# An encoder layer on one core: the second chunk's projection takes its weight quarters two at a time

## Chip, cores, metric

One core of a Trainium2 chip. The metric is the device time of one execution of the whole kernel in microseconds, the median over runs. The engines are named as the profile names them: PE (TensorE; PEld its weight loads), ACT (ScalarE), DVE (VectorE), POOL (GpSimd), SP (SyncE, whose queue issues the DMAs).

## What is computed

One encoder layer on two groups of tokens (1024 prompt and 256 sample tokens, each group with 16 meta tokens ahead), model width 2048, all in float32:

```python
def encoder_layer(h, norm_w, w_in, q_norm_a, k_norm_a, q_norm_b, k_norm_b, rpb, w_out, rope_tabs):
    u = rms_norm(h, norm_w) @ w_in                       # 2048 -> 52 strips of 128 columns
    qa, ka, va, za, qb, kb, vb, zb = jnp.split(u, split_points(), axis=-1)
    qa = apply_axial_rope(rms_norm(qa, q_norm_a), rope_tabs)      # 8 heads
    ka = apply_axial_rope(rms_norm(ka, k_norm_a), rope_tabs)      # 2 key/value heads
    ya = global_gqa(qa, ka, va) * jax.nn.silu(za)
    qb, kb = rms_norm(qb, q_norm_b), rms_norm(kb, k_norm_b)       # 8 heads
    yb = neighbourhood_attention(qb, kb, vb, rpb) * jax.nn.silu(zb)
    return h + jnp.concatenate([ya, yb], axis=-1) @ w_out
```

## The kernel before

**Arithmetic.** A float32 product is made of three matmuls on operands that are split into a high and a low part: high by high, high by low, low by high. `split` does it for a weight tile: ACT casts `wr` to the high part `wh` (line 66), DVE subtracts it for the low part `wl` (line 67). Activations `x` are kept split in SBUF.

**Chunks.** The tokens go in two chunks. Chunk one (sample tokens and the first part of the prompt) is projected up to about 600 us, chunk two (the other 784 prompt tokens) from there to 1758 us, and the output projection with its own sums (`products`, lines 1070 to 1072, PSUM tile `pq`) follows to the end. Chunk two's tokens are two blocks: 512 tokens (tile `x`) and 272 (tile `xb`). Its projection shares PE with the attention: first the eight global heads (about 640 to 1310 us), then, from 1310 us on, the eight local (neighbourhood) heads, whose scores and values are hung in between the strips by `run_due`.

**Strips.** `project` makes one strip of 128 output columns of `w_in` (a key, query, value or gate strip of a head) by `strips(jobs, getx)`. The first strip of chunk two is a joint one, with two jobs (`KA`, `VA`); the others have one. The contraction over 2048 rows is 16 k-tiles, in four quarters `c` of `WCH` = 4 k-tiles. Per quarter SP loads 256 KB of weights into a `wr` buffer (pool `raw`), ACT makes `wh` (a cast or copy) and DVE makes `wl`; for strips whose low part was kept from chunk one, SP loads `wl` from DRAM (`wld`, line 210) instead. The pool `w` has four buffers of `wh` and four of `wl`, so four quarters fit. Then for each token block `b` twelve matmuls (4 k-tiles by 3) go into that block's PSUM tile `pp`: 12 with 512 columns and 12 with 272 in each quarter, four times per strip. In the last strip (`turn`) the 272 block goes first.

**Behind a strip.** Keys and queries are squared (`ms`, ACT, line 260), summed over partitions on POOL, scaled by a root (`rs_l`, `rs_r`) and stored to DRAM, from where `qfull` and `kfull` are read back. Values are scaled (`vt`, DVE, line 289) and transposed on PE (`tp`, line 540); these transposes are ordered behind a certain place of the next strip, told by `tie` = (quarter, block). `z` is the gate strip.

**What sets the order.** Tile's scheduler sets the order of each engine's instructions from its own model of time; each engine runs its list in that order. Buffers of a pool come free when their last reader is through. At the end of chunk two the first `ww` tiles (weights of the output projection, line 1037) and the first `yf` (attention outputs, line 987, in the `raw` pool) are loaded, cast and split into `wm` and `yh`/`yl`, on the same ACT, DVE and SP lists; `behind_v` orders the splits of the fifth to sixteenth `wm` behind the last `vt`.

Of the kernel before, what the change touches and what calls it, by code (L numbers as in the profile page):

```python
# [48 lines left out]
WCH = 4  # L49
# [10 lines left out]
class Kern:  # L60
# [131 lines left out]
    def strips(self, jobs, getx):  # L192


        nc, tc = self.nc, self.tc
        out = [[pool.tile([P, 512], F32, tag=tag, name="pp") for pool, tag in pools] for _, _, pools in jobs]
        for c in range(KT // WCH):
            ws = []
            behind = self.behind.pop(0) if self.behind else None
            for j, (s, _, _) in enumerate(jobs):  # L200
                wp = self.w if j < 2 else self.w1
                with tc.high_priority(offset=self.woff), tc.issue_after(behind) if behind else nullcontext():
                    w = self.raw.tile([P, WCH, P], F32, tag="raw", name="wr")
                    cuts = ((0, 1), (1, WCH)) if self.projected == 3 and c == 0 and not self.second else ((0, WCH),)
                    for i, e in cuts:
                        self.lastw = nc.sync.dma_start(w[:, i:e], self.io["w_in"][s][:, c * WCH + i:c * WCH + e, :]).ins
                    wh = wp.tile([P, WCH, P], F32R, tag="wh", name="wh")
                    wl = wp.tile([P, WCH, P], F32R, tag="wl", name="wl")
                    if self.second and s not in AGAIN:
                        nc.sync.dma_start(wl[:].bitcast(F32), self.wld[s][:, c * WCH:(c + 1) * WCH, :])  # L210
                        nc.scalar.copy(wh[:], w[:])
                    else:
                        for i, e in cuts:
                            self.lastsplit = self.split(wh[:, i:e], wl[:, i:e], w[:, i:e])
                            self.lasthi = self.hi
                ws.append((wh, wl))
                if not self.second and s not in AGAIN:
                    nc.sync.dma_start(self.wld[s][:, c * WCH:(c + 1) * WCH, :], wl[:].bitcast(F32))
            nb = len(jobs[0][1])
            for b in range(nb)[::-1] if self.turn else range(nb):  # L220
                for k in range(WCH):
                    kt = c * WCH + k
                    xh, xl = getx(kt)[b]
                    first, last = kt == 0, kt == KT - 1
                    for (wh, wl), ps, (_, blocks, _) in zip(ws, out, jobs):
                        p, n = ps[b], blocks[b][1]
                        nc.tensor.matmul(p[:, :n], wh[:, k, :], xh[:, :n], start=first, stop=False)  # L227
                        nc.tensor.matmul(p[:, :n], wh[:, k, :], xl[:, :n], start=False, stop=False)  # L228
                        self.lastmm = nc.tensor.matmul(p[:, :n], wl[:, k, :], xh[:, :n], start=False, stop=last).ins  # L229
                if self.turned and (c, b) == self.tie:  # L230
                    for i in self.turned:
                        tc.add_manual_dep(i, self.lastmm.name, mybir.DependencyInfo(
                            mybir.DependencyClass.NoSync, mybir.DependencyReason.DATA), reason="turned")
                    self.turned = []
            if c % 2:
                self.run_due()
        return out
# [527 lines left out]
    def chunk2(self):  # L765
# [20 lines left out]
        def k_strip(s, g, wc, rope):  # L786
            k, km = k_first(g)

            def evac(ps):
                for p, (o, n) in zip(ps, BL):  # L790
                    rp = (ct[:, o:o + n], st[:, o:o + n]) if rope else None
                    self.qk_evac(p, o, n, wc, rp, [(0, n, k[:, 0, C1P + o:C1P + o + n], k[:, 1, C1P + o:C1P + o + n])])
                return k, km
            return s, BL, evac

        def v_rows_of(s, g):

            def evac(ps):
                for p, (o, n) in zip(ps, BL):
                    self.rows_out(self.v_rows(p, o, n), n, self.vn[g], C1P + o)  # L800
            return s, BL, evac

        def v_tiles(g):

            h, l = (self.v.tile([P, 8, P], F32R, tag=f"v{i}", name="va", align_bytes=ALIGN) for i in range(2))
            nc.sync.dma_start(l[:].bitcast(F32), self.vn[g][:].rearrange("(t p) d -> p t d", p=P))
            nc.scalar.copy(h[:], l[:].bitcast(F32))
            nc.vector.tensor_tensor(out=l[:], in0=l[:].bitcast(F32), in1=h[:].bitcast(F32), op=ALU.subtract)
            return [(h[:, j, :], l[:, j, :]) for j in range(8)], self.load_vm(g)
# [12 lines left out]
        def q_strip(s, h, wc, rope):  # L822
            q = self.q.tile([P, 2, NP], F32R, tag="q", name="q", align_bytes=ALIGN)
            nc.sync.dma_start(q[:, :, :C1P].bitcast(F32), self.qd[h][:])

            def evac(ps):
                for p, (o, n) in zip(ps, BL):
                    rp = (ct[:, o:o + n], st[:, o:o + n]) if rope else None
                    self.qk_evac(p, o, n, wc, rp, [(0, n, q[:, 0, C1P + o:C1P + o + n], q[:, 1, C1P + o:C1P + o + n])])
                return q  # L830
            return s, BL, evac

        def z_strip(s, h):
            z = self.z.tile([P, NP], F32, tag="z", name="z")
            nc.sync.dma_start(z[:, :C1P], self.zd[h][:, :C1P])

            def evac(ps):
                for p, (o, n) in zip(ps, BL):
                    self.z_evac(p, o, n, [(0, n, z[:, C1P + o:C1P + o + n])])
                return z  # L840
            return s, BL, evac
# [39 lines left out]
        def run(h, q, z, k, v):  # L881
            (k, km), (v, vm) = k, v
            for b in range(4):
                c = slice(QB * b, QB * b + QB)
                keys = [(k[:, 0, o:o + P], k[:, 1, o:o + P]) for o in range(0, NP, P)]
                for _ in self.attend(q[:, :, c], z[:, c], keys, km, v, vm[:], self.yd[0][:, 2 * b:2 * b + 2, h, :]):
                    pass
# [51 lines left out]
        def fill(n):  # L939
            for _ in range(min(n, len(late))):  # L940
                pr(late.pop(0))

        for g in range(2):
            if g == 0:
                k, _ = pr(k_strip(KA, 0, kw, True), v_rows_of(VA, 0))
                self.tie = 0, 1
            else:
                k, = pr(k_strip(KA + g, g, kw, True))
                pr(v_rows_of(VA + g, g))
            v = v_tiles(g)  # L950
            for h in range(4 * g, 4 * g + 4):
                z, = pr(z_strip(ZA + h, h) + (((self.sp, "sp"),) if h == 0 else ()))
                q, = pr(q_strip(QA + h, h, qw, True))
                run(h, q, z, k, v)
                fill(FILL)
# [2 lines left out]
            f(0)  # L958
        self.due = iter(local_heads())
        fill(len(late) - 1)  # L960
        self.turn, self.tie = True, (1, 0)
        fill(1)
        load_z(NH - 1)
        self.due = iter([[(0, f, (NH - 1, b)) for f, b in ((values, n - 2), (scores, n)) if 0 <= b < 4] for n in range(6)])
# [381 lines left out]
```

## Time and profile before

| | |
|---|---|
| runs | 2155.97, 2157.99, 2158.89 us; median 2157.99 |
| the profiled execution | 2156.31 us, of which the span is 2154.5 |
| PE busy | 2147.4 us, 11745 matmuls |
| DVE, ACT, POOL busy | 1666.1, 1190.9, 524.0 us |
| mean clock granted to PE | 1.00 |

Times in the rows are us from the span's start. A row of the timeline gives start, length, engine, line, operation and tiles (out<-in), and in brackets how long the engine sat idle before it and what ended that. Matmuls overlap: one of 512 columns has a length of about 0.39 us, while the next starts 0.23 us later, so what a stretch costs PE is read from starts. A row of the waits gives the sum, the number and the longest. The prediction shows the lines that it uses.

### The profile page before, as it was taken

How to read it: one execution, taken by the hardware profiler on the slowest of the kernel's cores; microseconds unless marked ns; L12 is line 12 of the kernel's file. 1: busy time of each engine (PE TensorE's matmuls, PEld its weight loads, DVE VectorE, ACT ScalarE, POOL GpSimd, SP SyncE). 2: the span in 40 equal slices, each digit the busy share in tenths (PEclk: the TensorE clock that was granted, in tenths of full speed). 3: DMA queues.
4: the chain of work that ended last, by engine and by line, in shares of the span. 5: the costliest groups of instructions: out<-in, count | busy, mean ns of one | idle time of the engine just before them, and what ended most of it. 6: DMA issues, size and time to landing. Idle time of an engine off the chain costs nothing.

```text
span 2154.5 us, 34001 instructions
## 1 busy us (share of the span) xinstructions
PE 2147.4 (100%) x11745; PEld 1878.4 (87%) x11745; DVE 1666.1 (77%) x3013; ACT 1190.9 (55%) x2419; POOL 524.0 (24%) x250
## 2 busy tenths in 40 slices
PE   9999999999999999999999999999999999999999
PEld 7888888888888999998999999989999888888887
DVE  7698977788874899996799988777787786545763
ACT  7677644454665777776677775444444454232230
POOL 1142422222221223231133224333333311000000
PEclk9999999999999999999999999999999999999999
DMA  8666789988654333334233244554433364762663
GB/s 294 215 193 220 238 291 320 341 280 281 212 191 133 97 102 106 110 97 142 91 110 100 95 129 150 184 161 135 138 124 123 114 215 140 242 234 91 234 225 107
DMA packets 257420, 377.24 MB, mean 175 GB/s; under 512 B 43072, under 2 KB 108768, under 8 KB 257248
## 3 DMA queue, kind: packets, MB, share of 16 engines
q1 hardware_dynamic: 257248, 375.07, 53.7%
q8 instruction: 92, 1.51, 0.3%
q14 instruction: 80, 0.66, 0.1%
HBM read 281.01 MB, written 100.38 MB: 177 GB/s over the span
## 4 chain that ended last, share of the span: by engine, by line
PE 98%; DVE 1%; DMA 1%; SPq 0%; issue 0%; ACT 0%; DVEq 0%
PE pp L229 22%; PE pp L227 22%; PE pp L228 22%; PE pq L1072 6%; PE pq L1070 6%; PE pq L1071 6%; PE po L519 2%; PE sp L485 2%; PE sp L378 1%; PE sp L379 1%; PE po L420 1%; PE sp L377 1%; PE po L419 1%; PE po L418 1%; PE tp L540 0%; PE sm_ps L316 0%
## 5 line engine op out<-in xcount | busy, mean ns | idle before, releaser
L227 PE MATMUL pp<-x,wh 128*128 128x512 f32 (+1 forms) x1664 | 654.0, 394 | 0.6 <-ACT wh L66 0.3
L229 PE MATMUL pp<-x,wl 128*128 128x512 f32 (+1 forms) x1664 | 647.8, 390 | 0.2 <-DVE wl L67 0.2
L228 PE MATMUL pp<-x,wh 128*128 128x512 f32 (+1 forms) x1664 | 647.9, 390 | 0.0
L229 PEld LDWEIGHTS pp<-x,wl 128*128 128x128 f32 x1664 | 312.5, 188 | 61.4 <-DVE wl L67 0.8
L227 PEld LDWEIGHTS pp<-x,wh 128*128 128x128 f32 x1664 | 312.4, 188 | 55.6 <-ACT wh L66 2.0
L228 PEld LDWEIGHTS pp<-x,wh 128*128 128x128 f32 x1664 | 312.9, 188 | 51.9
L262 POOL PARTITION_ALL_REDUCE m<-ms x78 | 223.1, 2860 | 352.5 <-ACT ms L260 300.3
L67 DVE TENSOR_TENSOR wl<-wr,wh 128x512 fp32r<-128x512 f32 (+2 forms) x287 | 209.6, 732 | 107.2 <-ACT wh L66 80.4
L346 POOL PARTITION_ALL_REDUCE tot<-a x80 | 181.0, 2262 | 433.5 <-DVE a L343 419.8
L66 ACT CAST wh<-wr 128x512 fp32r<-128x512 f32 (+2 forms) x287 | 173.5, 611 | 162.5 <-PE pp L228 147.8
L228 PE MATMUL pp<-xb,wh 128*128 128x272 f32 x832 | 240.8, 289 | 0.0
L227 PE MATMUL pp<-xb,wh 128*128 128x272 f32 x832 | 239.6, 288 | 0.0
L229 PE MATMUL pp<-xb,wl 128*128 128x272 f32 x832 | 239.0, 287 | 0.0
L328 POOL PARTITION_ALL_REDUCE ma<-m x80 | 113.3, 1417 | 447.8 <-DVE m L326 436.3
L1072 PE MATMUL pq<-wm,yl 128*128 128x512 f32 x560 | 218.3, 390 | 0.6 <-DVE yl L67 0.6
L1070 PE MATMUL pq<-wm,yh 128*128 128x512 f32 x560 | 218.3, 390 | 0.0
L1071 PE MATMUL pq<-wm,yh 128*128 128x512 f32 x560 | 218.0, 389 | 0.0
L227 PEld LDWEIGHTS pp<-xb,wh 128*128 128x128 f32 x832 | 156.5, 188 | 7.5
L228 PEld LDWEIGHTS pp<-xb,wh 128*128 128x128 f32 x832 | 156.5, 188 | 7.4
L229 PEld LDWEIGHTS pp<-xb,wl 128*128 128x128 f32 x832 | 157.4, 189 | 0.1
L1072 PEld LDWEIGHTS pq<-wm,yl 128*128 128x128 f32 x560 | 105.1, 188 | 22.9 <-DVE yl L67 1.0
L1071 PEld LDWEIGHTS pq<-wm,yh 128*128 128x128 f32 x560 | 105.1, 188 | 21.6
(218 smaller groups left out, 3951.9 us busy)
## 6 DMA issues: line engine op xcount, KB each, us to landing
wr<-in_w_in SPq DMA_DIRECT2D x413, 256.0 KB, 3.5
wld<-wl SPq DMA_DIRECT2D x132, 256.0 KB, 4.3
wl<-wld SPq DMA_DIRECT2D x132, 256.0 KB, 3.1
yr<-yd SPq DMA_DIRECT2D x35, 512.0 KB, 5.2
wq<-in_w_out SPq DMA_DIRECT2D x64, 256.0 KB, 5.1
td<-wq SPq DMA_DIRECT2D x64, 256.0 KB, 4.4
ww<-td SPq DMA_DIRECT2D x64, 256.0 KB, 5.2
ww<-in_w_out SPq DMA_DIRECT2D x48, 256.0 KB, 5.1
```

What stands on the lines that cost most here:

```text
L66: self.hi = nc.scalar.copy(hi, full).ins
L67: return nc.vector.tensor_tensor(out=lo, in0=full, in1=hi.bitcast(F32), op=ALU.subtract).ins
L227: nc.tensor.matmul(p[:, :n], wh[:, k, :], xh[:, :n], start=first, stop=False)
L228: nc.tensor.matmul(p[:, :n], wh[:, k, :], xl[:, :n], start=False, stop=False)
L229: self.lastmm = nc.tensor.matmul(p[:, :n], wl[:, k, :], xh[:, :n], start=False, stop=last).ins
L262: nc.gpsimd.partition_all_reduce(m2[:], ms[:], P, RED.add)
L328: nc.gpsimd.partition_all_reduce(ma[:], m1[:], P, RED.max)
L346: nc.gpsimd.partition_all_reduce(tot[:], a1[:], P, RED.add)
L485: nc.tensor.matmul(dst, k[:, o:o + P], qfv[:, a:e, :], start=True, stop=True)
L1070: nc.tensor.matmul(ps, yh, wh, start=k == 0, stop=False)
L1071: nc.tensor.matmul(ps, yh, wl, start=False, stop=False)
L1072: self.lastmm = nc.tensor.matmul(ps, yl, wh, start=False, stop=k == 7).ins
```

## The change

With one job and more than one token block, an even quarter of a strip only loads its weights and is held; the odd quarter that follows runs both: 24 matmuls for the first block with the two quarters' weights one after the other, then 24 for the second. `tie` is renamed to the pair in which the transposes are to come, since a pair counts by its first quarter.

```diff
         out = [[pool.tile([P, 512], F32, tag=tag, name="pp") for pool, tag in pools] for _, _, pools in jobs]
+        held = []
         for c in range(KT // WCH):
...
+            held.append((c, ws))
             nb = len(jobs[0][1])
+            if nb > 1 and len(jobs) == 1 and c % 2 == 0:
+                continue
             for b in range(nb)[::-1] if self.turn else range(nb):
-                for k in range(WCH):
-                    kt = c * WCH + k
+                for kt, ws in [(d * WCH + k, w) for d, w in held for k in range(WCH)]:
+                    k = kt % WCH
                     xh, xl = getx(kt)[b]
...
-                if self.turned and (c, b) == self.tie:
+                if self.turned and (held[0][0], b) == self.tie:
...
+            held = []
             if c % 2:
                 self.run_due()
         return out
...
-                self.tie = 0, 1
+                self.tie = 0, 0
...
-        self.turn, self.tie = True, (1, 0)
+        self.turn, self.tie = True, (0, 0)
```

Lines of the changed kernel stand five further down behind the edit (line 289 is 294, 540 is 545, 1037 is 1042), and the three matmul lines 227 to 229 are 231 to 233. The order of every engine's instructions is built anew. Each engine has as many of them as before.

The order of PE in one of the first strips (`pp_8007` is its 512 block, `pp_8008` its 272 block; `wh_8011`, `wl_8012` are quarter nought), at the end of that quarter's 512s. Before:

```order
L227 MATMUL pp_8007<-x_6761,wh_8011 128x512
L228 MATMUL pp_8007<-x_6761,wh_8011 128x512
L229 MATMUL pp_8007<-x_6761,wl_8012 128x512
L227 MATMUL pp_8008<-xb_6738,wh_8011 128x272
L228 MATMUL pp_8008<-xb_6738,wh_8011 128x272
L229 MATMUL pp_8008<-xb_6738,wl_8012 128x272
```

And after:

```order
L231 MATMUL pp_8007<-x_6761,wh_8011 128x512
L232 MATMUL pp_8007<-x_6761,wh_8011 128x512
L233 MATMUL pp_8007<-x_6761,wl_8012 128x512
L231 MATMUL pp_8007<-x_6769,wh_8017 128x512
L232 MATMUL pp_8007<-x_6769,wh_8017 128x512
L233 MATMUL pp_8007<-x_6769,wl_8018 128x512
```

The 512s of quarter one (`wh_8017`) follow at once, and the 272s of quarter nought come after them.

The order of DVE in the last strip, between the scaling of the value strip's first block (`vt_20168`) and that of its second (`vt_20178`); `q_20090` is the last query head's split, `wl_20262` is quarter two of the last strip, `wl_20292` (before) and `wl_20268` (after) quarter three, `wm` are output weights. Before:

```order
L67 TENSOR_TENSOR wl_20262<-wr_20259,wh_20261 128x512
L289 TENSOR_TENSOR vt_20168<-pp_20001,rb2_320 128x512
L355 TENSOR_TENSOR tot_19967<-tot_19967,r_20159 128x256
L356 SCALAR_TENSOR_TENSOR r_20159<-tot_19967,r_20159 128x256
L67 TENSOR_TENSOR q_20090<-qfull_20087,q_20090 128x1024
L67 TENSOR_TENSOR wl_20292<-wr_20289,wh_20291 128x512
```

And after:

```order
L294 TENSOR_TENSOR vt_20168<-pp_20001,rb2_320 128x512
L360 TENSOR_TENSOR tot_19967<-tot_19967,r_20159 128x256
L361 SCALAR_TENSOR_TENSOR r_20159<-tot_19967,r_20159 128x256
L67 TENSOR_TENSOR q_20090<-qfull_20087,q_20090 128x1024
L67 TENSOR_TENSOR wl_20262<-wr_20259,wh_20261 128x512
L67 TENSOR_TENSOR wl_20268<-wr_20265,wh_20267 128x512
```

The split of quarter two has moved behind the q split, whose cast ACT likewise does first now. Behind these rows four `wm` splits and then `vt_20178` follow in both.

The order of SP there. Before:

```order
L868 DMA qfull_20087<-q2d15_164 128x784
L987 DMA yf_20352<-yd0_165 128x512
L364 DMA yd1_166<-y_20074 128x4x64
L568 DMA vm3_271<-vmd9_98 48x128
L1037 DMA ww_20355<-in_w_out 128x512
```

And after:

```order
L873 DMA qfull_20087<-q2d15_164 128x784
L369 DMA yd1_166<-y_20074 128x4x64
L573 DMA vm3_271<-vmd9_98 48x128
L992 DMA yf_20352<-yd0_165 128x512
L1042 DMA ww_20355<-in_w_out 128x512
```

`yf_20352` goes into the raw buffer that the split `wl_20262` frees, and the first output weights stand behind it in both.

The order of PE at the transposes of the value strip's second block (`tp_20181`), in the last strip. Before:

```order
L229 MATMUL pp_20190<-x_6825,wl_20262 128x512
L227 MATMUL pp_20191<-xb_6834,wh_20291 128x272
L540 MATMUL tp_20181<-ident_239,vt_20178 128x128 x2
L540 MATMUL tp_20181<-ident_239,vt_20178 16x128
L228 MATMUL pp_20191<-xb_6834,wh_20291 128x272
```

And after:

```order
L233 MATMUL pp_20191<-xb_6858,wl_20268 128x272
L231 MATMUL pp_20190<-x_6801,wh_20261 128x512
L545 MATMUL tp_20181<-ident_239,vt_20178 128x128 x2
L545 MATMUL tp_20181<-ident_239,vt_20178 16x128
L232 MATMUL pp_20190<-x_6801,wh_20261 128x512
```

They stood behind the first 272 of quarter three, and stand now behind the first 512 of the second pair, whose twenty-four 272s come ahead of it.

## The prediction

> **What bounds the kernel now.** I read the page first: busy shares, then the chain that ended last. TensorE (PE) is busy all the time, and 98% of the chain is PE, two thirds of it the projection's three matmul lines. So the time moves only if PE's matmuls come closer together or if PE waits.
>
> ```profile
> PE 2147.4 (100%) x11745; PEld 1878.4 (87%) x11745; DVE 1666.1 (77%) x3013; ACT 1190.9 (55%) x2419; POOL 524.0 (24%) x250
> ...
> PE 98%; DVE 1%; DMA 1%; SPq 0%; issue 0%; ACT 0%; DVEq 0%
> PE pp L229 22%; PE pp L227 22%; PE pp L228 22%; PE pq L1072 6%; PE pq L1070 6%; PE pq L1071 6%; PE po L519 2%; PE sp L485 2%; PE sp L378 1%; PE sp L379 1%; PE po L420 1%; PE sp L377 1%; PE po L419 1%; PE po L418 1%; PE tp L540 0%; PE sm_ps L316 0%
> ```
>
> Then the stretches of PE alone (us, busy with count, clock, DMA share, GB/s). The first two are chunk two: PE busy without a gap at full clock. The third is the output projection, 1325 matmuls of 512 columns in 300.00 us, so 226.4 ns each: the step of an undisturbed run of 512s.
>
> ```profile
> 640.00:1310.00 670.00, 670.00 (x4316) 1.00 0.36 109
> 1310.00:1757.00 447.00, 447.00 (x2688) 1.00 0.46 147
> 1830.00:2130.00 300.00, 300.00 (x1325) 1.00 0.57 198
> ```
>
> Then the waits. From 640 to 1757 us no wait of PE is listed, so inside the strips nothing can be won by bringing data earlier; from 1757 on PE has one. Of the other engines the waits that touch the change are those for a weight slot: SP's and ACT's, which end when PE has used up the quarter that sat there.
>
> ```profile
> PE pq L1072 <- DVE yl L67: 0.6, 1, 0.6
> SPq L210 <- PE pp L229: 341.4, 117, 7.0
> ACT wh L66 <- PE pp L228: 147.8, 96, 4.4
> ```
>
> **The change part by part.** It adds and removes no instruction; 100 pairs of quarters (50 strips of two pairs; the joint strip and chunk one keep their order) run as 24 matmuls of 512 columns and 24 of 272 in place of 12, 12, 12, 12.
>
> *Matmul order.* The place shown in the order lists is 669.53 to 678.02 us in the trace, a pair without attention in it. The joint strip before it already runs 24 and 24, which is a trial of the new order inside this trace (start, modelled length):
>
> ```profile
> 626.36 0.39 PE L227 MATMUL pp<-x,wh 128*128 128x512 f32 x1
> ...
> 631.80 0.29 PE L227 MATMUL pp<-xb,wh 128*128 128x272 f32 x1
> ...
> 634.79 0.40 PE L227 MATMUL pp<-x,wh 128*128 128x512 f32 x1
> ...
> 637.53 0.29 PE L227 MATMUL pp<-xb,wh 128*128 128x272 f32 x1
> ...
> 669.53 0.39 PE L227 MATMUL pp<-x,wh 128*128 128x512 f32 x1
> ...
> 672.28 0.29 PE L227 MATMUL pp<-xb,wh 128*128 128x272 f32 x1
> ...
> 673.78 0.39 PE L227 MATMUL pp<-x,wh 128*128 128x512 f32 x1
> ...
> 678.02 0.39 PE L227 MATMUL pp<-x,wh 128*128 128x512 f32 x1
> ```
>
> Differences of starts: the pair in the present order takes 8.49 us (669.53 to 678.02). Its twelve 512s take 2.75, twelve undisturbed ones 12 x 0.2264 = 2.72: a run of 512s that is entered from 272s loses 0.03 us in its first steps. The twelve 272s take 1.50. In the joint strip 24 and 24 take 8.43 (626.36 to 634.79): 5.44 and 2.99. The run of 512s behind it, entered after twenty-four 272s, takes 2.74, so a longer run of 272s doesn't make the entry dearer. A pair with one entry less should take 2.75 + 2.72 + 2.99 = 8.46, 0.03 less than now; taken whole from the joint strip it is 8.43, 0.06 less.
>
> How many entries go? Counted through the built order of PE, passages from a 272 to a 512 of the projection fall from 156 to 58, since in pairs with attention the attention's matmuls often stand between; passages from attention into a 512 fall from 158 to 126, and into a 272 rise from 129 to 168. The 98 are worth 98 x 0.03 = 2.9 us. For the 32 I have no row that isolates the loss, so I bound it by nothing and by the same 0.03 (1.0 us) and take 0.4. Term: -3.3 us; ends -2.9 and, with the joint strip's 0.06 on all 100 pairs, -6.
>
> The Trainium skill, "TensorE: Matmul & The Clock Gate", section "Back-to-back issue gap", gives an isolated spacing of N/2.4 + 2.5 ns, whatever stands before: 216 ns for 512 columns and 116 for 272. By it a pair would take 24 x (216 + 116) = 7.97 us in either order and this term would be zero; the trace disagrees in the size (8.49) and in that the same twelve 512s take 2.75 or 2.72.
>
> *Weight slots.* Four quarters fit. An even quarter is now held until its 272s are through at 5.45 + 1.50 = 6.95 us of the pair instead of 4.25, so its slot comes free 2.7 us later; an odd one at 8.5 as now, but it is first needed 2.72 us into the pair and not at 4.25, 1.5 us sooner. SP, which waits there 341.4 us with loads of keys, values and later weights queued behind, and ACT, with softmax steps behind a cast, wait up to 2.7 us longer. How early weights stand ready: quarter two of the last strip, whose low half is split by 1741.25 (row below), is first used one pair after the strip's start at 1740.61, near 1749, so 7.7 us early; read by name, the other quarters of chunk two are 6.8 to 20 us early. 2.7 + 1.5 = 4.2 leaves 2.6 at worst. Cost nothing, as long as that margin covers it; if it doesn't, PE waits for `wl`.
>
> *PSUM.* The same two banks per strip are written over the same pair; the 512 bank is finished 3.0 us before the strip's end and not 1.5, so its evacuation can start sooner. Nothing.
>
> *Transposes.* Behind a pair's first 24 matmuls in place of a quarter's 24 they come 5.4 us after a strip's start instead of 4.2. Their readers are copies and a store of value rows, needed a strip later. Nothing, except in the last strip.
>
> *Last strip and handover to the output projection*, the one place where the order of work moves (start, length, engine; waits in brackets). ACT, then SP, DVE and PE:
>
> ```profile
> 1728.27 0.63 ACT L77 ACTIVATE rs_l<-m 128x512 f32<-128x512 f32 x1 [3.22 <-DVE m L263]
> 1729.40 0.24 ACT L561 CAST km<-kfull 128x64 fp32r<-128x64 f32 x1 [0.49 <-DMA kfull<-kfd]
> ...
> 1730.20 0.40 ACT L260 ACTIVATE ms<-pp 128x272 f32<-128x272 f32 x1
> ...
> 1745.62 1.05 ACT L66 CAST q<-qfull 128x1024 fp32r<-128x1024 f32 x1 [1.81 <-DMA yf<-yd]
> ...
> 1748.11 0.62 ACT L66 CAST wm<-ww 128x512 fp32r<-128x512 f32 x1 [0.92 <-PE pp L229]
> 1748.93 1.87 ACT L66 CAST wm<-ww 128x512 fp32r<-128x512 f32 x3 [0.20 <-DMA ww<-in_w_out]
> ```
>
> ```profile
> 1742.74 0.38 SPq L987 DMA_DIRECT2D yf<-yd  x1
> ...
> 1744.20 6.08 SPq L1037 DMA_DIRECT2D ww<-in_w_out  x5
> ```
>
> ```profile
> 1740.58 0.67 DVE L67 TENSOR_TENSOR wl<-wr,wh 128x512 fp32r<-128x512 f32 x1
> ...
> 1746.70 1.23 DVE L67 TENSOR_TENSOR q<-qfull,q 128x1024 fp32r<-128x1024 f32 x1 [1.91 <-ACT q L66]
> 1747.84 0.69 DVE L67 TENSOR_TENSOR wl<-wr,wh 128x512 fp32r<-128x512 f32 x1
> ...
> 1749.24 2.49 DVE L67 TENSOR_TENSOR wm<-ww,wm 128x512 fp32r<-128x512 f32 x4
> 1751.65 0.43 DVE L289 TENSOR_TENSOR vt<-pp,rb 128x272 f32<-128x272 f32 x1
> ...
> 1761.72 0.68 DVE L67 TENSOR_TENSOR yl<-yf,yh 128x512 fp32r<-128x512 f32 x1
> ```
>
> ```profile
> 1740.61 0.42 PE L227 MATMUL pp<-xb,wh 128*128 128x272 f32 x1
> ...
> 1754.11 0.49 PE L540 MATMUL tp<-ident,vt 128*128 128x128 f32 x3
> ...
> 1761.48 0.39 PE L1071 MATMUL pq<-wm,yh 128*128 128x512 f32 x1
> 1762.45 0.50 PE L1072 MATMUL pq<-wm,yl 128*128 128x512 f32 x1 [0.59 <-DVE yl L67]
> 1762.79 0.39 PE L1070 MATMUL pq<-wm,yh 128*128 128x512 f32 x1
> ```
>
> Now: the last strip starts at 1740.61. Quarter two's low weights are split at 1740.58, ahead of the long q split; the raw buffer that this frees lets SP load `yf` at 1742.74 and, behind it in SP's queue, the output weights (`ww`) at 1744.20. Four of them are cast by 1750.80 (6.6 us after the first issue) and split, `vt` ends at 1752.08, and the transposes that read it run at 1754.11, 2 us later: cover that the change uses up.
>
> After: the low split stands behind the q split, `yf` and `ww` behind the low split, `vt` behind four `wm` splits. If q arrives as now, the q split ends at 1747.93, the low one 0.69 later at 1748.6 (PE wants it one pair into the strip, 1740.61 + 8.43 = 1749.0, so it is just in time), `yf` goes then and `ww` 0.45 behind at 1749.05; plus 6.6 to the fourth cast, 0.6 for its split, 0.43 for `vt`: 1756.7. The transposes stand one pair (8.43), 24 matmuls of 272 (2.99), one of 512 (0.23) and four earlier transposes (0.5) behind the strip's start: 1752.8. PE would stand 3.9 us. But ACT's order now puts the square `ms` of the last query strip's second block ahead of the key cast `km`, which waits for a transfer and delays it by 0.6 us (idle 0.49 before 1729.40, and 0.15 to the next start), and DVE's sum `m` of the first block, for which ACT stands 3.22 us until 1728.27, is one place forward. So the chain from that square to q (sum over partitions, root, store, reload, cast) starts earlier: by nothing, or by 0.6 and half of that 3.22, 2.3 together (an estimate). That bounds the stall by 1.6 and 3.9 with `ww` landing as now; with landings as short as the shortest of this kind it shrinks by some 1.2 (2.6 for the 3.8 us of the first one here):
>
> ```profile
> DMA to landing us min/median/max: 2.6/5.1/8.4
> ```
>
> Ends 0.4 and 3.9; I take 1.2, nearer the low one, since the whole chain from that square follows it. Against it stands the one wait of PE: the step from 1761.48 to 1762.45 is 0.97 for 0.227, the next 0.34, together 0.86 lost to a `yl` that DVE split at 1761.72 behind a row of `wm`. The last Z block's 272s now end 2.7 us sooner against the strip's end, so its scaling clears DVE sooner; I take this wait as gone. Handover: 1.2 - 0.9 = +0.3, ends -0.5 and +3.9.
>
> *Sum* against the profiled execution's 2156.31 us (span 2154.5 and 1.8 around it): -3.3 + 0.3 = 2153.3. The median of the runs, 2157.99, is 1.7 above that execution, so 2155.0 for the median.
>
> **The rivals.**
>
> C, larger gain: the whole 0.06 to 0.07 of the joint strip on every pair, and the wait gone: -6 to -7.5, with little of a stall. For it: the joint strip's 24 512s have no entry loss at all. Against: it has two jobs' weights in turn, and attention stands in half the other pairs. 2150.5 to 2152.
>
> A, a new wait in place of the old: q arrives as now and PE stalls 3.9 us at the transposes in the last strip, with the wait at 1762.45 gone or not: -3.3 + 3.9 - 0.4 = +0.2, 2158.2. For it: every link stands in the order. Against: ACT's order starts the chain sooner.
>
> B, no gain: the loss at entry is made up by something else, or the 272s gain what the 512s lose, so a step's mean depends on the columns alone. 0 + 0.3: 2158.3. Against: 2.75 and 2.72 in the trace. The Trainium skill's formula named above would give this result.
>
> D, slower: ACT is held at a weight cast 2.7 us longer, with a softmax step of the global heads behind it, and values come to PE late. It decides as soon as that step has less than 2.7 us of cover. 32 global blocks (8 heads of 4); if one in four loses half of 2.7, 8 x 1.35 = 10.8, less 3.0: 2165.8. For it: ACT waits there 96 times already. Against: no wait of PE in 1117 us, and ACT is busy 55%.
>
> **How the numbers follow.** The three runs spread over 0.14%; 0.2%, 4.3 us, is about what a measurement of this kernel can tell from no change. Forecast 0.48 (2153 to 2157), C 0.20, A 0.14, B 0.10, D 0.08. Faster than 2153.7 are C and a lower edge of the forecast, 0.06: 0.26. Slower is D: 0.08. The rest is same: 0.66. The range takes the forecast, A, B and the near half of C: 2151.5 to 2159.
>
> **What would show it.** The pair at 669.53 takes 8.46 us or a little less; chunk two from 640 to its end is 3 us shorter with PE still 100% busy; no PE wait before 1740; one on `vt` of about 1 us at the last strip's transposes; none on `yl`. I am wrong if entries into 512 still cost what they did per pair, if PE waits for `wl`, softmax or value operands inside strips, or if the `vt` wait is near 4 us.

## The result: slower by 0.16%

The changed kernel takes 2160.32 us (median of 22 runs, 2158.29 to 2163.36) against 2157.02 before (22 runs, 2155.94 to 2160.07): a ratio of 1.0016, 95% interval 1.0011 to 1.0022. The forecast was 2155.0 in a range of 2151.5 to 2159. The profiled executions differ by 4.0 us of span, 2158.5 against 2154.5.

The changed kernel's page, shares and chain. PE's busy time fell by 0.9 us, its share to 99%, and 5% of the chain left PE, for DVE, issue and ACT:

```profile
PE 2146.5 (99%) x11745; PEld 1879.5 (87%) x11745; DVE 1674.9 (78%) x3013; ACT 1188.1 (55%) x2419; POOL 512.6 (24%) x250
...
PE 93%; DVE 3%; issue 1%; ACT 1%; DMA 1%; POOL 0%; SPq 0%; DVEq 0%; POOLq 0%; ACTq 0%
```

Its waits of PE after 600 us, where there had been one of 0.6:

```profile
PE tp L545 <- DVE vt L294: 2.7, 1, 2.7
PE po L521 <- DVE Pm L343: 1.6, 1, 1.6
PE po L425 <- DVE pl L67: 0.8, 2, 0.4
```

PE at the pair whose price the prediction worked out:

```profile
669.40 0.40 PE L231 MATMUL pp<-x,wh 128*128 128x512 f32 x1
...
674.87 0.29 PE L231 MATMUL pp<-xb,wh 128*128 128x272 f32 x1
...
677.86 0.40 PE L231 MATMUL pp<-x,wh 128*128 128x512 f32 x1
```

The pair takes 8.46 us (before 8.49), 5.47 and 2.99, as worked out. PE around the last two strips, starts again, waits in brackets:

```profile
1738.05 0.29 PE L233 MATMUL pp<-xb,wl 128*128 128x272 f32 x1
1739.91 0.36 PE L521 MATMUL po<-Pm,vm 128*128 128x256 f32 x1 [1.57 <-DVE Pm L343]
...
1753.19 0.40 PE L231 MATMUL pp<-x,wh 128*128 128x512 f32 x1
1756.32 0.87 PE L545 MATMUL tp<-ident,vt 128*128 128x128 f32 x3 [2.74 <-DVE vt L294]
1756.85 0.78 PE L232 MATMUL pp<-x,wh 128*128 128x512 f32 x1
1757.42 0.63 PE L233 MATMUL pp<-x,wl 128*128 128x512 f32 x1
1757.85 0.63 PE L231 MATMUL pp<-x,wh 128*128 128x512 f32 x1
```

Two waits, and behind the second the 512s start 0.43 us apart, not 0.227. The stretch of PE from 1756 to 1760 gives the granted clock as 0.57:

```profile
1756.00:1760.00 4.00, 3.68 (x11) 0.57 1.03 368
```

So the slow steps, five of 0.43 behind one of 0.57, go with a lowered clock, and no wait is listed for them. The Trainium skill, "TensorE: Matmul & The Clock Gate", section "Part 1: The HAM clock gate", states that it falls to half after about 3.4 us of idle; the traces disagree: here 2.74 us were enough, and in three of the runs below about 1.9.

Where 4.0 us come from, by starts of matmuls in both traces (chunk two and output projection, 1550.32 us before and 1554.30 after): the strips up to 1721 us are 2.40 shorter in their steps (the 512s 2.98 shorter, the attention's matmuls 0.60 longer); the two waits on `pl`, a low half of the probabilities, cost 1.09; the wait on `Pm` 1.73; that on `vt` 2.91; the slow steps behind it, those of the transposes with them, 1.53; the rest of the handover is 0.88 shorter, 0.75 of it the lost step on `yl`, which is gone. Sum +4.0.

What the wait on `vt` hangs on (DVE, then SP, then ACT):

```profile
1739.35 0.41 DVE L343 TENSOR_TENSOR Pm<-Sm,Pm 16x256 fp32r<-16x256 f32 x1
...
1746.48 1.23 DVE L67 TENSOR_TENSOR q<-qfull,q 128x1024 fp32r<-128x1024 f32 x1 [2.06 <-ACT q L66]
1747.62 1.29 DVE L67 TENSOR_TENSOR wl<-wr,wh 128x512 fp32r<-128x512 f32 x2
...
1752.45 0.69 DVE L67 TENSOR_TENSOR wm<-ww,wm 128x512 fp32r<-128x512 f32 x1 [2.75 <-ACT wm L66]
...
1755.74 0.43 DVE L294 TENSOR_TENSOR vt<-pp,rb 128x272 f32<-128x272 f32 x1
```

```profile
1748.34 0.32 SPq L992 DMA_DIRECT2D yf<-yd  x1
1748.75 4.75 SPq L1042 DMA_DIRECT2D ww<-in_w_out  x9
```

```profile
1751.80 0.62 ACT L66 CAST wm<-ww 128x512 fp32r<-128x512 f32 x1 [4.31 <-DMA ww<-in_w_out]
```

The q split is 0.2 us sooner than before, not 2.3; from there on each link is where the prediction's upper end had it, and `vt` ends at 1756.2 for 1756.7. `Pm` ends at 1739.8 where it ended at 1738.6 before the change, while PE wants it at 1738.2. Before the change PE took it at 1739.5, 0.9 us after it was ready; that was its cover:

```profile
1738.17 0.41 DVE L338 TENSOR_TENSOR Pm<-Sm,Pm 16x256 fp32r<-16x256 f32 x1
```

```profile
1739.53 0.28 PE L516 MATMUL po<-Pm,vm 128*128 128x256 f32 x1
```

### The profile page after: what moved, and what is told of

It is laid out like the page before. It is cut to its first block, busy times and chain, and to the rows that moved or that the text cites. A ratio compares the mean times of both kernels' runs of the same rounds, so it can differ in the third digit from the quotient of the medians.

```text
span 2158.5 us, 34003 instructions
## 1 busy us (share of the span) xinstructions
PE 2146.5 (99%) x11745; PEld 1879.5 (87%) x11745; DVE 1674.9 (78%) x3013; ACT 1188.1 (55%) x2419; POOL 512.6 (24%) x250
## 4 chain that ended last, share of the span: by engine, by line
PE 93%; DVE 3%; issue 1%; ACT 1%; DMA 1%; POOL 0%; SPq 0%; DVEq 0%; POOLq 0%; ACTq 0%
PE pp L232 21%; PE pp L231 21%; PE pp L233 21%; PE pq L1077 6%; PE pq L1076 6%; PE pq L1075 6%; PE po L524 2%; PE sp L490 2%; PE po L425 1%; PE sp L383 1%; PE sp L382 1%; PE sp L384 1%; PE po L424 1%; PE po L423 1%; PE tp L545 0%
## 5 line engine op out<-in xcount | busy, mean ns | idle before, releaser
L351 POOL PARTITION_ALL_REDUCE tot<-a x80 | 169.4, 2118 | 436.6 <-DVE a L348 407.2
L1076 PEld LDWEIGHTS pq<-wm,yh 128*128 128x128 f32 x560 | 105.2, 188 | 21.8
L1075 PEld LDWEIGHTS pq<-wm,yh 128*128 128x128 f32 x560 | 105.1, 188 | 21.7
```

Of the source, the lines that this page charges most:

```text
L351: nc.gpsimd.partition_all_reduce(tot[:], a1[:], P, RED.add)
L1075: nc.tensor.matmul(ps, yh, wh, start=k == 0, stop=False)
L1076: nc.tensor.matmul(ps, yh, wl, start=False, stop=False)
```

## Experiments

Theory 1: the step gain is real, and the new order of the lists of DVE, ACT and SP at the end of chunk two makes the loss. Theory 2: the pairs themselves make it, since PE asks sooner than the others can follow. Beside the timing (ratio to before with its interval), "from 600" is the time from the first matmul on `xb` to the last start on `pq` in the profiled execution, 1550.32 before and 1554.30 after; it leaves out chunk one, whose end lies between 599.7 and 601.4 us in these traces. Strips of chunk two are numbered from 0 (the joint one) to 50 (the last). All kernels that pair only some strips have this edit, with `tie` as before in the others:

```diff
-            if nb > 1 and len(jobs) == 1 and c % 2 == 0:
+            if pair and c % 2 == 0:      # pair: PAIRS(number of the strip)
```

**Which strips.** The last one quarter by quarter (`n < 50`), the last two (`n < 49`), and the last one alone in pairs (`n == 50`):

> All strips of chunk two in pairs except the last one, which goes quarter by quarter as before. In the built order the low split of the last strip's quarter two still stands behind the long q split on DVE, with the attention-output load and the output weights behind it on SP, and the meta probabilities (Pm) still stand behind a weight split of the next strip; only the transposes are back behind the first 272 of quarter three. Theory 1 (the lists of DVE and SP make the loss at the end): the wait on Pm stays at about 1.6 us and the transposes still wait, some 1.2 to 1.8 us, since their place is 1.2 us later and the value scaling as late as in the changed kernel; time about 1 us above before, 2158. Theory 2 (the pair in the last strip makes the loss by asking for the transposes sooner): no wait at the transposes, time about 2156.

> All strips in pairs except the last two. In the built order the low split of the last strip's quarter two stands ahead of the q split again, as before the change. Both theories: no wait at the transposes and no slow clock behind it. Theory 1: the wait on Pm goes too or falls under 0.5 us; what is left is the gain of the matmul order, 2.2 us, less two waits of 0.44 us on a low half of the probabilities (pl) among the global heads: 2155.5 to 2156, 1 to 1.5 us below before. The rival that the entry into a run of 512s costs nothing and the gain in the trace is noise: 2157 or above.

> Only the last strip in pairs, all others quarter by quarter as before. In the built order the low split of its quarter two stands ahead of the q split, the transposes stand where they do in the changed kernel. Theory 1: the value scaling ends near 1752.1 us as before and the transposes, wanted near 1752.8, wait under 0.5 us; the wait of 0.86 us on the low half of y is gone: between 0.9 us below before and no change, 2156 to 2157. Theory 2: the transposes wait 2 to 3 us and the clock falls behind them: 3 us above before, 2160.

| | time, us | ratio | from 600 |
|---|---|---|---|
| last strip apart | 2159.86 | 1.0008 (0.9999 to 1.0017) | 1553.52 |
| last two apart | 2158.30 | 0.9999 (0.9991 to 1.0008) | 1550.55 |
| last alone in pairs | 2155.87 | 0.9992 (0.9983 to 1.0000) | 1549.88 |

Waits of PE after 600 us in the first:

```profile
PE po L524 <- DVE Pm L346: 1.9, 1, 1.9
PE tp L548 <- DVE vt L297: 1.3, 1, 1.3
PE pq L1080 <- DVE yl L68: 1.1, 2, 0.9
PE po L428 <- DVE pl L68: 0.8, 2, 0.4
```

and in the second:

```profile
PE po L524 <- DVE Pm L346: 1.8, 1, 1.8
PE po L428 <- DVE pl L68: 0.8, 2, 0.4
```

In the third none is listed. With the last strip apart the transposes still wait, 1.3 us, inside the bounds of theory 1 (the time is 2.0 us above before for its 1, since `yl` is late again and `Pm` later); with the last strip alone in pairs, and its transposes where the changed kernel has them, they don't wait at all. So the pair in the last strip isn't what makes that wait. Counted from the first matmul on `xb`, `vt` ends at 1156.2 us in the changed kernel and with the last strip apart, at 1152.7 with the last two apart, at 1152.6 with the last alone, and at 1152.1 before the change. What the three have in common with the lists: the low split of quarter two stands behind the q split where strip 49, the one before, is paired, and ahead of it where it is not. A paired strip holds the weight buffer that quarter two needs until near its end; this is the link that the prediction's section on slots had costed at nothing. That the held buffer is why the scheduler moved the row is read from the lists and not shown by a run. The expectation that the wait on `Pm` goes with the second was wrong: it stays, 1.8 us, and the gain in steps (the strips up to the last two are 2.4 us shorter there, waits apart) is spent on it and on `pl`. Seven of the eleven executions of the second have a mean granted clock of 0.999 and take 2157.6 to 2158.6 us; the other four, the profiled one among them, have 1.000 and take 2156.5 to 2157.5. So its median is longer than its trace would have it.

**The opposite dose.** No pairs, and each quarter goes through its blocks in two halves:

```diff
-            for b in range(nb)[::-1] if self.turn else range(nb):
-                for kt, ws in [(d * WCH + k, w) for d, w in held for k in range(WCH)]:
+            parts = ((0, 2), (2, 4)) if self.second and len(jobs) == 1 else ((0, WCH),)
+            for b, (ka, kb) in [(b, p) for p in parts for b in (range(nb)[::-1] if self.turn else range(nb))]:
+                for kt, ws in [(d * WCH + k, w) for d, w in held for k in range(ka, kb)]:
```

> The opposite dose: no pairs, and each quarter of chunk two's single strips goes through its blocks in two halves (6 of 512, 6 of 272, 6, 6), which raises the passages from a 272 into a 512 from 156 to 322. Theory that an entry into a run of 512s costs about 0.03 us, 0.027 of it in the first six steps: 166 x 0.027 = 4.5 us more, 2161.5, with the quarter at 4.28 us for 4.25 where no attention stands between. Rival that a step's mean depends on the columns alone: no change, quarter 4.25 us.

2164.20 us, 1.0028 (1.0017 to 1.0038), from 600 1558.25. A quarter without attention takes 4.27 us:

```profile
669.48 0.40 PE L235 MATMUL pp<-x,wh 128*128 128x512 f32 x1
...
673.75 0.40 PE L235 MATMUL pp<-x,wh 128*128 128x512 f32 x1
```

The 512s together are 2.8 us longer, 0.017 for each of the 166 entries more, where 0.027 was expected; only the first three steps of a run are long here (233, 236, 236 ns), as in the changed kernel. Most of the rest are waits of PE, the longest this one:

```profile
PE sm_ps L324 <- DVE mx L396: 1.4, 1, 1.4
```

So both doses move the 512s the way the entries go, up with more and down with fewer, and the rival that columns alone count falls. The price of an entry isn't one number: 0.017 us for each one added here, 0.030 for each of the 98 taken away (2.98).

**The clock.** Twelve spare matmuls in the place where PE stood:

```diff
+                        if self.nth == 50 and kt == 8 and b == 0:
+                            fp = self.pp.tile([P, 512], F32, tag="pp", name="fill")
+                            for _ in range(12):
+                                j = nc.tensor.matmul(fp[:], wh[:, k, :], xh[:], start=True, stop=True).ins
...
```

> The changed kernel with twelve spare matmuls of 512 columns (2.7 us of PE) between the last strip's first 512 and the transposes that wait for the value scaling; their result is not used. They fill the 2.74 us in which PE stood. Theory that PE's clock fell because PE stood still: the transposes wait 0.3 us or less and the matmuls behind them start 0.227 us apart, not 0.427; 1.2 to 1.5 us less than the changed kernel, 2159. Rival that the slow steps come from what follows the transposes (late weights, PSUM) or that the clock doesn't look at PE's standing: steps of 0.427 stay, no change, 2160.3.

2159.61 us, 1.0014 (1.0006 to 1.0023), from 600 1554.54. The stretches of PE around the wait on `Pm` and around the transposes:

```profile
1738.00:1745.00 7.00, 5.11 (x27) 0.76 0.57 164
1755.00:1765.00 10.00, 10.00 (x47) 1.00 1.04 361
```

Behind the filled place the clock stays at 1.00 and no step of 0.427 is left, so it was PE's standing still that had lowered it. But nothing was won in this execution: its wait on `Pm` is 1.9 us and the clock fell there instead (0.76). PE came 1.3 us later to the filled place for that, so without the spare matmuls it would have stood there some 1.9 us and not 2.7 (an estimate from the end of `vt`). Over all executions the fall became rarer: a mean granted clock of 0.999 or less in 19 of 22 of the changed kernel, in 3 of 11 here. The medians lie 3.3 and 2.7 us above before, so 0.6 of the expected 1.2 to 1.5 showed, within the intervals.

**Moving single rows.** Cast and split of the last strip's quarter two ahead of q; then also `Pm` ahead of two rows of DVE; then the two strips with a wait on `pl` (6 and 20) without pairs; then cast and split also ahead of the last block's root steps:

```diff
+                            if self.nth == 50 and c == 2:
+                                self.place_after(self.lastq[0], self.lastsplit, "q late")
+                                self.place_after(self.lastq[1], self.hi, "q late")
...
+                                self.place_after(self.lastsplit, self.lastpm, "pm first")
...
+                self.place_after(i, self.lastpm, "pm first")
...
+                                self.place_after(self.lastr[0], self.hi, "r late")
+                                self.place_after(self.lastr[1], self.lastsplit, "r late")
```

> The changed kernel with one row moved on DVE, one on ACT and one on SP: cast and split of the last strip's quarter two stand ahead of cast and split of q, as before the change, and the attention-output load goes ahead of a store and a value load on SP. PE's order is that of the changed kernel. Theory 1 (this row makes the stall): value scaling ends near 1752 us, no wait over 0.5 us at the transposes, no slow steps; the wait on Pm (1.7 us) and the two on the probabilities' low half (0.5 each) stay: 2.9 + 1.3 less, at most 0.9 back for a late low half of y: 2156 to 2157. Rival that the pairs alone make it (PE asks for the transposes 1.2 us sooner and DVE is full): the wait stays at 2 us or more, 2159 to 2160.

> As the kernel before it, and on DVE the meta probabilities (Pm) of the last block ahead of the split of the next strip's odd quarter and of the last scaling of the query strip, two rows further. Theory that the order on DVE makes the wait on Pm: Pm ends 1.0 to 1.2 us sooner, the wait falls from 1.7 to 0.5 or 0.7 us, 1.0 to 1.2 less than the kernel before it: 2155 to 2156. Rival that DVE is full there and PE's lead of 1.3 us is simply paid back: the wait stays over 1.2 us or comes back at the next place, no change.

> As the kernel before it, without pairs in the two strips (of the first and the second key group) in whose last quarter PE waited 0.5 us each for the probabilities' low half. Theory that these waits come from the pair in that strip: both gone, 1.0 us less, 0.14 lost of the gain: 2154 to 2155, and about 2.5 us below before. Rival that PE's lead from other strips makes them: they stay or move, no change.

> As the kernel with both rows moved, and cast and split of the last strip's quarter two also ahead of the last local block's logarithm on ACT and its product on DVE, as before the change; three rows of ACT and five of DVE differ from the changed kernel. Theory (what was still late is this cast, which stood behind a step that waits for a sum on POOL until 1743): split near 1741, output weights near 1744, value scaling by 1752; the transposes wait 0.3 us or less for 2.0; the wait on Pm stays at 1.0; from 600 us to the end 1549.3 to 1550.2 us for 1551.5, so no more than before the change (1550.3), and 2156 to 2157. Rival (the slot that the pair of the strip before holds until its end delays the cast wherever it stands): cast at 1741 or later, the transposes still wait over 1 us.

| | time, us | ratio | from 600 | wait on Pm | on vt |
|---|---|---|---|---|---|
| split ahead of q | 2157.85 | 1.0005 (0.9996 to 1.0014) | 1551.89 | 1.9 | none |
| and Pm ahead | 2157.74 | 1.0007 (0.9998 to 1.0015) | 1551.46 | 1.0 | 2.0 |
| and 6 and 20 apart | 2157.68 | 1.0002 (0.9993 to 1.0011) | 1550.69 | 1.0 | 1.7 |
| split ahead of q and roots, Pm ahead | 2156.96 | 0.9998 (0.9989 to 1.0007) | 1550.51 | 0.8 | 1.2 |

One row moved on each of three engines, with PE's list untouched, takes 2.4 us of the 4.0 back (by the medians 2.4 of 3.3). In the profiled execution, at 2159.24 us the longest of the eleven, no wait on `vt` is left, and no slow step behind it. PE's waits after 600 us, the stretch of PE behind the wait on `Pm`, and `vt`:

```profile
PE po L527 <- DVE Pm L349: 1.9, 1, 1.9
PE po L431 <- DVE pl L68: 0.8, 2, 0.4
```

```profile
1739.00:1747.00 8.00, 6.05 (x35) 0.79 0.41 129
```

```profile
1755.70 0.43 DVE L300 TENSOR_TENSOR vt<-pp,rb 128x272 f32<-128x272 f32 x1
```

But theory 1 holds only in part. `vt` ends at 1756.1 and not near 1752; counted from the first matmul on `xb` that is 1154.8 us, for 1156.2 in the changed kernel and 1152.1 before, so the row gives back 1.4 of 4.1. That PE doesn't wait for it comes also of the 1.8 us more that PE had lost at `Pm`, where the clock fell (0.79). With `Pm` ahead as well PE comes in time, `vt` ends at the same 1154.8, and 2.0 us of wait are back. So the stall has two makers: the lists make `vt` late, as theory 1 has it, and PE's lead decides how much of that PE waits, as theory 2 has it.

What still held the split was its cast, which stood behind a root step that waits for POOL (ACT, split ahead of q and `Pm` ahead):

```profile
1743.03 0.42 ACT L368 ACTIVATE r<-tot 128x256 f32<-128x256 f32 x1 [4.25 <-POOL tot L361]
1743.48 0.42 ACT L369 ACTIVATE r<-r 128x256 f32<-128x256 f32 x1
1743.81 0.61 ACT L67 CAST wh<-wr 128x512 fp32r<-128x512 f32 x1
```

Moved ahead of that too, the cast runs at 1739.4 without a wait, so the held slot that the rival named doesn't delay it. The wait over 1 us that the rival forecast came even so: 1.2 us on `vt` for the 0.3 expected, the split ending at 1744.5 and not near 1741. DVE is nearly full up to there; its busy time from 1731 to 1744.5 us is the figure with x28, 13.10 of 13.50 us (before the change 11.20):

```profile
1731.00:1744.50 13.50, 12.69 (x82) 11.56 (x81) 13.10 (x28) 6.11 (x16) 5.93 (x3) 1.00 0.41 133
```

Part of that is the run's own, its chunk one ending 0.9 us later. And the split is no longer all that holds the load of `yf`: in SP's list it stands right behind q's reload, which goes at 1744.2 (counted from the first matmul on `xb`, 0.9 later than before the change):

```profile
1744.21 0.32 SPq L885 DMA_DIRECT2D qfull<-q2d  x1
1744.62 0.38 SPq L1004 DMA_DIRECT2D yf<-yd  x1
```

What was taken off one wait came back for the most part at the next (`Pm` ahead: 2.4 us less up to the end of strip 49, by a wait 0.9 shorter and no fall of the clock, and 2.0 more on `vt`). The waits on `pl` did go with the pairs of their own strips.

**All of it, and stopping early.** The last of these with 6 and 20 apart and both splits of the first pair behind `Pm`; pairs up to strip 45 but for 6 and 20, with the lists at the end as before the change; and pairs in strips 33 to 45 and 50 only:

> All that helped together: the kernel before it, without pairs in the two strips where PE waited for the probabilities' low half, and with both splits of the last strip's first pair behind Pm on DVE. Theory: no wait on the low half, Pm's wait 0.5 to 0.8 us, none at the transposes; from 600 us to the end 1548.2 to 1549 us, 1.3 to 2.1 us below before the change; 2155 to 2156, at the edge of what the timing tells. Rival that PE's lead is paid back wherever DVE or POOL are full: 1550 or more.

> Pairs in the strips of chunk two up to the last five, but not in the two with a wait on the probabilities' low half; the last five strips go quarter by quarter, and the order lists of DVE, ACT, SP and PE at the end are those of before the change. Theory (the lists make the waits at the end): Pm's wait 0.6 us or less, since it had 1.3 us of cover and PE leads by 1.9; none at the transposes; from 600 us to the end 1548.4 to 1549.3 us for 1550.3: 1.0 to 1.9 us below before, 2155 to 2156. Rival (DVE is full and any lead of PE is paid back there): Pm's wait 1.5 us or more, 1550 or above, no change.

> Pairs only in thirteen strips under the local heads, ahead of the last five, and in the last strip. Theory: 13 x 0.07 = 0.9 us from the matmul order, which stays within the cover at Pm, and 0.4 from the wait on the low half of y, as in the kernel with the last strip alone; at most 0.4 of wait at the transposes: from 600 us to the end 1548.9 to 1549.5 us, 2156. Rival as above: the lead comes back as waits on Pm or the transposes, 1550 or above.

| | time, us | ratio | from 600 |
|---|---|---|---|
| all together | 2158.82 | 1.0006 (0.9997 to 1.0015) | 1553.71 |
| stop early | 2157.16 | 0.9998 (0.9989 to 1.0007) | 1550.95 |
| under local heads, and the last | 2156.16 | 0.9995 (0.9986 to 1.0004) | 1551.90 |

The first was a miss: the splits that were pushed back came late, PE waited 0.6 us for one of them and 1.9 at the transposes, and the clock fell again. PE's waits after 600 us in the second:

```profile
PE pq L1080 <- DVE yl L68: 1.1, 2, 0.9
PE po L524 <- DVE Pm L346: 0.4, 1, 0.4
PE tp L548 <- DVE vt L297: 0.2, 1, 0.2
PE sp L385 <- DVE mx L395: 0.2, 1, 0.2
```

With the old lists at the end the wait on `Pm` is 0.4, as theory 1 had it (0.6 or less), and the one on `vt` lies in strip 32, not at the last transposes. The lead of PE, 1.2 us at 1720, is nonetheless gone: 0.6 in the step at `Pm`, then 1.45 in steps on `yl` in the handover, for 0.75 before the change. The second of these isn't PE's lead being paid back: with the same lists the low half `yl` ends 0.6 us later than before the change (1163.0 and 1162.4 from the first matmul on `xb`), behind an output weight that landed later:

```profile
1757.32 0.62 ACT L67 CAST wm<-ww 128x512 fp32r<-128x512 f32 x1 [1.25 <-DMA ww<-in_w_out]
```

So the time came out as the rival had it, 1550 or above, but its reason is seen only in the 0.6 at `Pm`. The third has its 0.88 us in the thirteen local strips (0.9 expected), and lost 2.1 in strips 12 and 14 under the global heads (with waits of 0.3 and 0.6), in a stretch whose lists are those of before; such margins change from run to run, and the profiled execution, 2157.60 us, is the second longest of the eleven. No version is faster than before by more than its interval; the last strip alone in pairs comes nearest, and its gain in the trace, 0.44, is on `yl`.

## Why the prediction was wrong

The forecast added -3.3 for the matmul order and +0.3 for the last strip and handover. The traces have -2.4 and +6.4. The step that failed is the second: a stall of 1.2 at the transposes was to be nearly all that the new order of work costs, and in its place stand 2.91 there, 1.73 on `Pm`, 1.09 on `pl` and 1.53 of slow steps, less the 0.88 of the handover.

- *Matmul order, -3.3.* The mechanism was right, the size off: the pair takes 8.46 as worked out, the 512s fell by 2.98 us. What the term left out is the attention's matmuls, 0.60 longer in the new neighbourhood; -2.40 in all, outside the stated ends of -2.9 and -6.
- *The handover as "the one place where the order of work moves".* This failed. The lists also changed ahead of `Pm`, in strip 49, where the scaling of the query strip and one weight split now stand before it on DVE (1.73 us), and under the global heads (`pl`, 1.09). I had looked at the waits of PE before, none, and took the absence of a wait for cover; it was 0.9 us at `Pm`, while PE came 1.35 sooner and `Pm` 1.2 later.
- *Weight slots, "cost nothing".* This failed too, though PE didn't wait for weights after 600 us. The price wasn't late weights but the list, which a buffer held 2.7 us longer is likely to have changed: where strip 49 is paired, the split of quarter two stands behind q, and with it stand `yf`, `ww` and `vt`.
- *The stall at the transposes.* Every link was named and the ends were 0.4 and 3.9; it was 2.9, and PE had lost 1.7 at `Pm` on its way there, without which it would have stood longer. The choice of 1.2 rested on the q chain starting sooner by up to 2.3 us, and q came 0.2 sooner: the query strip's square ran at 1730.0 for 1730.2, since the root steps ahead of it were as late as before. With the upper end the sum would have been 2157.7 (2155.0 and 2.7 more), still 2.6 below the measured time. One reading was off besides: before the change `yf` went not when the split freed its buffer (1741.25) but right behind q's reload on SP, so q's chain set it, and the moved split changed what it hangs on:

```profile
1742.33 0.32 SPq L868 DMA_DIRECT2D qfull<-q2d  x1
```

- *The clock* was in no term: 1.5 us of slow steps behind a wait of 2.7.
- *`yl`, -0.9*: the number came, 0.75 and 0.88 with the step behind it, but in good part by luck. The low half ends 2.5 us later than before (1164.9 and 1162.4 from the first matmul on `xb`), and PE doesn't wait for it because PE comes 4.9 us later itself. Where PE comes on time, in the kernel with the last strip alone in pairs, the low half ends 0.5 sooner, and 0.45 of the 0.86 is won.
- *Rivals.* A was the nearest and had 0.14; it lacked the clock and the two other places. D, the only one to be called slower, named the global heads and ACT; what came there was 1.1 us, on DVE.

## What to carry over

When PE is busy all the time, a faster matmul order helps only as far as the engines behind it have cover; read that cover (when the operand is ready, when PE wants it) at the places where PE would wait first, since a list of waits that is empty doesn't tell it. A buffer that is held longer can also change the order that a scheduler builds: compare the lists of all engines, not only at the place that seems to matter, and look at what stands ahead of each operand that PE takes. In this kernel the last 40 us of chunk two are set by DVE, ACT and the loads as much as by PE, so 2.4 us won before them could not be kept.

## Of the hardware

- Where no attention stands between, a run of 512-column matmuls that follows 272-column ones starts with three steps of about 233, 236 and 236 ns, then 227, in the changed kernel and in the halves; before the change, in runs of twelve, the excess lay over the first seven (228 to 236). Other patterns occur too. Over the first six steps the excess above 226.6 ns a step sums to 0.023 to 0.024 us on average in all three kernels (runs of six and more: 110 before, 42 in the changed kernel, 247 in the halves).
- PE's clock fell behind some waits of about 2 us and not behind others: no fall at steps lengthened by 1.7 us (changed kernel, `Pm`), 1.9 (6 and 20 apart, `vt`), 2.0 (last two apart, and last apart, both `Pm`) and 2.1 (`Pm` ahead, at `vt`); a fall at 2.05 (filled, `Pm`; all together, `vt`), 2.1 (split ahead of q, `Pm`) and 2.9. In the run with all together a wait of 0.6 had ended 1.4 us before. Between 2.0 and 2.2 us the length alone didn't decide, nor did the kernel (mean clock 1.000 in four executions of the last two apart, 0.999 in seven); what does stays open.
